# Delta rule in a scheduled two-layer kernel: key norms of four heads at once, one decay matrix per head, norms folded into columns

## Chip, cores and metric

One core of a Trainium2 chip. The metric is the device time of one execution in microseconds (us); lower is better.

## What is computed

Two layers on x of shape 512 x 2048, all in float32. Layer 0 is chunked attention beside an mLSTM; layer 1 is an RG-LRU beside a gated delta rule with 8 heads of width 128. The change touches the delta rule alone, which in the reference is (chunks of 64 there, the kernel uses chunks of 128):

```python
qkv = silu(causal_dwconv(concatenate([qd, kd, vd]), conv_d_w))
q, k = l2norm(q), l2norm(k)                     # x * rsqrt(sum(x*x) + 1e-6)
decay = cumsum(gc)                              # per chunk and head
gam = exp(where(tril, decay[t] - decay[s], NEG))
a_mat = where(strict, (k*beta)[t] . k[s] * gam, 0)
t_inv = inverse(eye + a_mat)
u, w = t_inv @ (v*beta), t_inv @ (k*beta*exp(decay))
qk = q[t] . k[s] * gam
kd = k * exp(decay[-1] - decay)
# scan over chunks: v_new = u - w@st; o = (q*exp(decay))@st + qk@v_new
#                   st = exp(decay[-1])*st + kd^T@v_new
```

## The kernel before

Every product runs on TensorE (PE) with each float32 operand split into a high and a low part, so that a product of two operands is three matmuls (lines 291 to 293, or 365 in the paired form). Layer 1 multiplies the normed input by 48 tiles of weights; each tile is 16 steps of such a triple. The program is recorded by hand in the order in which it is to run on PE, VectorE (DVE), ScalarE (ACT) and GpSimd (POOL): `Net.run` walks through units of four steps, and beside each it issues, ahead of their use, the loads of raw weights (10 units ahead, on SP's queue), the split of the weights (5 units ahead: ACT rounds to the high part, line 247, DVE subtracts, line 248) and the matmuls. After every two steps, that is six matmuls, it calls `tick`, and a tick advances each active job by one step:

```python
def tick(self):
    while len(self.active) < self.nact and self.jobs:
        self.active.append(self.jobs.popleft())
    for g in list(self.active):
        if next(g, self) is self:
            self.active.remove(g)
```

Jobs are generators that emit their instructions on all engines and then wait a number of ticks from the table LAG (`yield from self.wait("gam")`). So places in the program are counted in ticks, and each engine runs its own list in order.

The jobs of layer 1 stand in a queue (lines 1039 to 1048), of which four are active until the solve is done, then six (line 1224):

- `start1`: the norm of the rows, the gates, and `delta_gates`, which leaves columns of decay, exp(decay), exp(last decay - decay) and beta per head in `cols`.
- `delta_keys(h)`, eight of them: convolution of the keys (line 1137, three DVE operations), silu, transposes on PE (1165), the sum of squares by head (1173), a reciprocal root by Newton steps on 128x4 columns (`rsqrt_cols`, lines 623 to 629), the decay matrix with a strict triangle in `gamma` (two POOL operations 1149 and 1150, one Exp on ACT 1152), a product by a column on POOL (1188), k.k on PE (1193), the product with the decay matrix on DVE (1194), and a write of the result to DRAM (`ud`, line 1195, issued by POOL).
- `solve`: loads 32 pieces of `ud` of all heads (1207, on SP's queue), and inverts the 32x32 diagonal blocks of all heads at once by 31 steps of one product (1214) and one sum (1220) on DVE, the last on 961 elements per partition. It waits `sv`, 8 ticks, between loads and first step.
- `lru_block(n)`: the RG-LRU of one block: convolution, parts (595, 1356), six matmuls, then a chain over ACT and DVE with a scan (1378) and a gate (672, 1380).
- `inverse(h)`: blocks from the solve are put together (DVE transpose 1242, matmuls 1250 and 1257, copies); `kd` is scaled on POOL (1241).
- `delta_head(h)`: q and v convolved, a second decay matrix `att` (POOL 1278, 1279, ACT 1282, POOL 1284), q.k (1291), transpose of v (1297), then the scan over four chunks (1310 to 1329), norm and gate.

DVE thus holds, in one list, the splits that PE's next weights need (248) and the work of all jobs.

Of the kernel before, what the change touches and what calls it, by code (L numbers as in the profile page):

```python
# [52 lines left out]
for _h in range(4):  # L53
# [14 lines left out]
    "sums": 1, "sums.x0": 40, "sums.y0": 14, "sums.y1": 10, "ml.sm": 2, "vals": 4,  # L68
    "conv": 2, "gam": 8, "sv": 8,
    "sv.n": 300,  # L70
# [10 lines left out]
class Net:  # L81
# [9 lines left out]
    def __init__(self, ctx, tc, a):  # L91
# [31 lines left out]
        self.spilt = {}  # L123
        self.heads = self.turn = 0
        self.paired = {"x0", "y0", "y1"}
# [607 lines left out]
    def start0(self, raw):  # L733
# [19 lines left out]
        yield from self.lam_scale()  # L753
        self.tri1 = self.triangle(-NEG, -1)
        yield from self.wait(4)
# [259 lines left out]
    def layer1(self):  # L1015
# [23 lines left out]
        self.jobs += [self.start1()]  # L1039
        self.jobs += [self.delta_keys(h) for h in range(8)]  # L1040
        self.jobs += [self.solve()]
# [11 lines left out]
    def start1(self):  # L1053
        while ("x1", KT - 1) not in self.t and ("x1", KT - 1) not in self.x:
            yield
        self.phase.close()
        self.mp = self.phase.enter_context(self.tc.tile_pool(name="m1", bufs=1))
        self.nact = 4
        self.cols = self.mp.tile([P, 4, 4, 8], F32, name="dcols")
        self.ncols = self.mp.tile([P, 4, 8], F32, name="ncols")  # L1060

        self.kcols = self.mp.tile([P, 8, 4, 4], F32, name="kcols")
        yield from self.wait("row1")
        yield from self.row_norm(self.acc)
        g = self.gate_rows((yield from self.take("g1")))
        yield from self.delta_gates(g)
# [24 lines left out]
    def delta_gates(self, g):  # L1091
# [52 lines left out]

    def gamma(self, h, db, g, tri):

        nc = self.nc
        yield
        nc.gpsimd.tensor_tensor(self.c4(g), self.c4(db), self.mask_bc(tri), ALU.subtract)
        nc.gpsimd.tensor_tensor(self.c4(g), self.c4(g), self.col_bc(self.cols[:, 0, :, h]), ALU.subtract)  # L1150
        yield from self.wait("gam")
        nc.scalar.activation(g, g, AF.Exp)
        yield

    def delta_keys(self, h):
        nc = self.nc
        cv = yield from self.take((h, "k"))
        k = yield from self.conv(cv, C_DW + 32 + 4 * h)
        yield from self.wait("dk.silu")
        yield from self.silu2(k)  # L1160
        yield from self.wait("dk.tr")
        nc.gpsimd.dma_start(self.kfd[h], k)
        ps = self.psum("dk.tr")
        for c in range(4):
            nc.tensor.transpose(ps[:, c * P : c * P + P], k[:, c * P : c * P + P], self.ident)
        kt, g = self.ev(), self.ev()
        sq = self.tmp()
        nc.scalar.activation(kt, ps, AF.Copy)
        ss = self.small(P, 4)
        nc.scalar.activation(sq, kt, AF.Square)  # L1170
        db = self.dec_bc(h)
        yield from self.wait(2)
        nc.vector.tensor_reduce(ss, self.c4(sq), AX.X, ALU.add)
        nc.gpsimd.dma_start(self.ktd[h], kt)
        while "gates1" not in self.t:
            yield

        nc.vector.tensor_scalar(ss, ss, 4 * EPS, None, ALU.add)
        r = self.rsqrt_cols(ss)
        kc = self.kcols[:, h]  # L1180
        nc.vector.tensor_copy(kc[:, 0], r)
        nc.vector.scalar_tensor_tensor(kc[:, 1], ss, 0.5, r, ALU.mult, ALU.mult)
        nc.vector.tensor_tensor(kc[:, 2], r, self.cols[:, 3, :, h], ALU.mult)
        nc.vector.tensor_tensor(kc[:, 3], r, self.cols[:, 2, :, h], ALU.mult)
        nb = self.small(P, 4)
        nc.vector.scalar_tensor_tensor(nb, kc[:, 2], -1.0, r, ALU.mult, ALU.mult)
        yield from self.gamma(h, db, g, self.tri1)
        nc.gpsimd.tensor_tensor(self.c4(g), self.c4(g), self.col_bc(nb), ALU.mult)
        yield from self.wait("dk.kk")
        ps = self.psum("dk.kk")  # L1190
        for c in range(4):
            kc = k[:, c * P : c * P + P]
            nc.tensor.matmul(ps[:, c * P : c * P + P], kc, kc, start=True, stop=True)
        nc.vector.tensor_tensor(g, g, ps, ALU.mult)
        nc.gpsimd.dma_start(self.ud[h], g)
        self.t[(h, "u")] = True
# [29 lines left out]
    def inverse(self, h):  # L1226
# [13 lines left out]
        yield from self.wait("inv.tp")  # L1240
        nc.gpsimd.tensor_tensor(self.c4(kd), self.c4(kd), self.col_bc(self.kcols[:, h, 3]), ALU.mult)
        nc.vector.transpose(l, x)
# [23 lines left out]
    def delta_head(self, h):  # L1266
# [7 lines left out]
        db = self.dec_bc(h)  # L1274
        kc = self.kcols[:, h]
        q = yield from self.conv(cq, C_DW + 4 * h, out=q)
        nc.scalar.activation(ed, db, AF.Exp)
        nc.gpsimd.tensor_tensor(self.c4(att), self.c4(db), self.mask_bc(self.tri), ALU.subtract)
        nc.gpsimd.tensor_tensor(self.c4(att), self.c4(att), self.col_bc(self.cols[:, 0, :, h]), ALU.subtract)
        v = yield from self.conv(cv, C_DW + 64 + 4 * h, out=v)  # L1280
        yield from self.wait("gam")
        nc.scalar.activation(att, att, AF.Exp)
        yield from self.silu2(q)
        nc.gpsimd.tensor_tensor(self.c4(att), self.c4(att), self.col_bc(kc[:, 0]), ALU.mult)

# [12 lines left out]
        vt = v  # L1298
        nc.vector.tensor_tensor(self.c4(vt), self.c4(ps), self.col_bc(kc[:, 1]), ALU.mult)
        x4, kd = yield from self.take((h, "inv"))  # L1300
# [5 lines left out]
        for c in range(4):  # L1306
# [10 lines left out]
            vn = self.small(P, P, "r", 6)  # L1317
            nc.vector.tensor_scalar(vn, ps[:, :P], kc[:, 2, c : c + 1], None, ALU.mult)
            yield from self.wait("dh.kv")
# [26 lines left out]
    def lru_block(self, n):  # L1346
        nc = self.nc
        cv = yield from self.take((n, "x"))
        gw = self.mp.tile([P, 256], F32, tag="gw", name=self.uid("gw"), bufs=1)
        gp = [self.mp.tile([P, 256], F32R, tag=t, name=self.uid(t), bufs=1) for t in ("gh", "gl")]  # L1350
# [144 lines left out]
```

## Time and profile before

| what | value |
|---|---|
| median of 3 runs | 1870.02 us (1868.22 to 1870.05) |
| the profiled execution | 1869.16 us, span of its instructions 1867.3 us |
| busy share | PE 98%, DVE 73%, ACT 47%, POOL 14% |
| layer 1 | from about 1050 us to the end |

The span runs from the first to the last instruction. A busy PE is one with a matmul in flight; how fast these follow each other is seen in the timeline, where the start of one to the start of the next is its cost.

### The profile page before, as it was taken

What the parts mean: (1) busy time and instruction counts of PE and PEld (TensorE: products, weight loads), DVE (VectorE), ACT (ScalarE), POOL (GpSimd) and SP (SyncE); (2) the same over time, 40 slices, a digit from 0 to 9 for tenths busy, and PEclk for the clock granted to TensorE, in tenths of its full rate; (3) what the DMA queues carried; (4) which work ended last, traced back from release to release, by engine and by line L of the source; (5) the groups of instructions that cost most, each with busy time, mean ns of one, the idle gap of its engine ahead of it and who ended that gap; (6) DMA issues with size and microseconds to landing.
All of it is one profiled execution on the core that took longest, in us unless ns stands there. A gap on an engine that the chain in (4) does not pass through costs nothing.

```text
span 1867.3 us, 27580 instructions
## 1 busy us (share of the span) xinstructions
PE 1833.3 (98%) x10162; PEld 1567.9 (84%) x10162; DVE 1358.4 (73%) x2352; ACT 868.7 (47%) x1512; POOL 264.7 (14%) x293
## 2 busy tenths in 40 slices
PE   7999999999999999999999999999999999999999
PEld 4789889989889899988899788887788888777998
DVE  8577747797647558788777799889656666768664
ACT  4346435645435355565434544363323334566332
POOL 8101100210110101011011114201212112100000
PEclk9999999999999999999999999999999999999999
DMA  5333423333433333325644435443433333245542
GB/s 184 100 106 109 134 87 119 96 113 116 135 100 106 115 102 108 113 86 187 222 141 149 147 118 169 146 119 103 150 93 114 110 114 110 75 124 166 175 136 74
DMA packets 137287, 232.12 MB, mean 124 GB/s; under 512 B 22896, under 2 KB 32240, under 8 KB 137152
## 3 DMA queue, kind: packets, MB, share of 16 engines
q1 hardware_dynamic: 129488, 208.60, 36.8%
q0 software_dynamic: 5360, 17.57, 2.5%
q10 hardware_dynamic: 2304, 4.20, 0.6%
q8 instruction: 80, 1.31, 0.3%
q14 instruction: 55, 0.45, 0.1%
HBM read 203.79 MB, written 26.51 MB: 123 GB/s over the span
## 4 chain that ended last, share of the span: by engine, by line
PE 78%; DVE 14%; issue 3%; ACT 2%; DMA 2%; SPq 1%; DVEq 0%; ACTq 0%
PE pp L365 38%; PE pp L291 8%; PE pp L293 7%; PE pp L292 7%; DVE act L248 3%; PE pp L427 3%; PE pp L429 3%; PE pp L428 3%; DVE act L1214 1%; ACT act L247 1%; DVE act L567 1%; DVE act L1137 1%; DVE ev L1137 1%; DMA act<-in_xT 1%; SPq L1207 0%
## 5 line engine op out<-in xcount | busy, mean ns | idle before, releaser
L365 PE MATMUL pp<-act,act 128*128 128x256 f32 (+1 forms) x4884 | 794.5, 322 | 0.0
L365 PEld LDWEIGHTS pp<-act,act 128*128 128x128 f32 x4884 | 707.0, 190 | 70.2
L248 DVE TENSOR_TENSOR act<-wr,act 128x512 fp32r<-128x512 f32 x719 | 521.6, 741 | 240.6 <-ACT act L247 237.0
L247 ACT ACTIVATE act<-wr 128x512 fp32r<-128x512 f32 x719 | 418.8, 620 | 200.7 <-DVE wr L222 61.5
L291 PE MATMUL pp<-act,act 128*128 128x512 f32 x960 | 390.3, 407 | 1.3 <-ACT act L563 1.3
L293 PE MATMUL pp<-act,act 128*128 128x512 f32 x960 | 378.1, 394 | 11.8 <-DVE act L248 11.6
L292 PE MATMUL pp<-act,act 128*128 128x512 f32 x960 | 376.9, 393 | 2.7 <-DVE act L567 1.9
L293 PEld LDWEIGHTS pp<-act,act 128*128 128x128 f32 x960 | 181.4, 189 | 54.1 <-DVE act L248 15.1
L291 PEld LDWEIGHTS pp<-act,act 128*128 128x128 f32 x960 | 182.1, 190 | 40.6 <-issue 3.8
L292 PEld LDWEIGHTS pp<-act,act 128*128 128x128 f32 x960 | 181.9, 189 | 38.9 <-DVE act L567 3.2
L427 PE MATMUL pp<-act,act 128*128 128x512 f32 x256 | 100.3, 392 | 0.0
L429 PE MATMUL pp<-act,act 128*128 128x512 f32 x256 | 99.7, 390 | 0.0
L428 PE MATMUL pp<-act,act 128*128 128x512 f32 x256 | 99.7, 389 | 0.0
L222 DVE TENSOR_TENSOR wr<-wr,wr 128x512 f32<-128x512 f32 x111 | 78.0, 703 | 1.3
L980 POOL TENSOR_SCALAR pq<-pq,mx 128x512 f32<-128x512 f32 (+3 forms) x32 | 47.4, 1495 | 188.7 <-DVE mx L977 188.7
L381 ACT ACTIVATE ee<-pp 128x512 f32<-128x512 f32 x74 | 44.0, 594 | 61.5 <-PE pp L365 61.3
L528 POOL DMA_DIRECT2D yd<-ev x20 | 11.4, 568 | 401.6 <-DVE ev L1011 164.5
L784 DVE TENSOR_TENSOR ev<-ev,pp 128x512 f32<-128x512 f32 x32 | 22.0, 687 | 47.6 <-PE pp L365 43.0
L429 PEld LDWEIGHTS pp<-act,act 128*128 128x128 f32 x256 | 48.0, 188 | 10.1
L428 PEld LDWEIGHTS pp<-act,act 128*128 128x128 f32 x256 | 48.1, 188 | 9.7
L427 PEld LDWEIGHTS pp<-act,act 128*128 128x128 f32 x256 | 48.1, 188 | 9.6
L593 ACT ACTIVATE act<-ev 128x512 fp32r<-128x512 f32 x40 | 24.9, 627 | 52.3 <-DVE ev L938 31.0
(334 smaller groups left out, 2033.1 us busy)
## 6 DMA issues: line engine op xcount, KB each, us to landing
wr<-in_wi SPq DMA_DIRECT2D x216, 256.0 KB
wr<-in_ws SPq DMA_DIRECT2D x100, 256.0 KB
wr<-in_wd SPq DMA_DIRECT2D x100, 256.0 KB
wr<-in_wv SPq DMA_DIRECT2D x64, 256.0 KB
wr<-in_wso SPq DMA_DIRECT2D x48, 256.0 KB
wr<-in_wdo SPq DMA_DIRECT2D x48, 256.0 KB
wr<-in_wo SPq DMA_DIRECT2D x32, 256.0 KB
ev<-x1d SPq DMA_DIRECT2D x28, 256.0 KB
```

Of the source, the lines that this page charges most:

```text
L222: sub = lambda o, x, y: nc.vector.tensor_tensor(o, x, y, ALU.subtract)
L247: nc.scalar.activation(h, w, AF.Copy)
L248: nc.vector.tensor_tensor(l, w, h.bitcast(F32), ALU.subtract)
L291: nc.tensor.matmul(ps, h[:, j, :], xh, start=k == 0, stop=False)
L292: nc.tensor.matmul(ps, h[:, j, :], xl, start=False, stop=False)
L293: nc.tensor.matmul(ps, l[:, j, :], xh, start=False, stop=k == KT - 1)
L365: mm = lambda o, x, y, start=False: nc.tensor.matmul(o, x, y, start=start, stop=True, skip_group_check=True)
L381: nc.scalar.activation(e, ps, AF.Copy)
L427: nc.tensor.matmul(ps, xh, h, start=k == 0, stop=False)
L428: nc.tensor.matmul(ps, xh, l, start=False, stop=False)
L429: nc.tensor.matmul(ps, xl, h, start=False, stop=k == KT - 1)
L980: nc.gpsimd.tensor_scalar(rows(b), rows(b), mx[:, 3, b : b + 1], None, ALU.mult)
```

## The change

Four things. The job `delta_keys` is cut in two, `keys(h)` and `couplings(h)`; between them stands `key_norms`, once for heads 0 to 3 and once for 4 to 7, which does the Newton steps on 128x16 columns of four heads. The decay matrix is made once per head: one POOL subtraction (1195), four Exps of 128x128 on ACT with the decay column as bias (1198), written to DRAM (`gd`) by POOL; `delta_head` loads it from there on SP's queue in place of making its own. The norms are no longer multiplied into matrices on POOL: they enter as columns, in four 128x128 DVE evictions of k.k (1207), and in column products that were there already; `kd` is scaled by four ACT operations. And `lru_block` waits until the block before it has issued its matmuls; the queue of jobs has a new order.

```diff
-    "conv": 2, "gam": 8, "sv": 8,
+    "conv": 2, "gam": 5, "dk.db": 3, "dh.q": 6, "sv": 8,
...
-        self.jobs += [self.delta_keys(h) for h in range(8)]
+        self.jobs += [self.keys(h) for h in range(4)] + [self.key_norms(0)]
+        self.jobs += [f(h + 4 * i) for h in range(4) for i, f in ((1, self.keys), (0, self.couplings))]
+        self.jobs += [self.key_norms(4)] + [self.couplings(h) for h in range(4, 8)]
...
+        nc.vector.tensor_scalar(self.ndec, self.cols[:, 0], -1.0, None, ALU.mult)
...
-    def gamma(self, h, db, g, tri):
-
-        nc = self.nc
-        yield
-        nc.gpsimd.tensor_tensor(self.c4(g), self.c4(db), self.mask_bc(tri), ALU.subtract)
-        nc.gpsimd.tensor_tensor(self.c4(g), self.c4(g), self.col_bc(self.cols[:, 0, :, h]), ALU.subtract)
-        yield from self.wait("gam")
-        nc.scalar.activation(g, g, AF.Exp)
-        yield
...
-        nc.vector.tensor_reduce(ss, self.c4(sq), AX.X, ALU.add)
+        nc.vector.tensor_reduce(self.kcols[:, 0, h], self.c4(sq), AX.X, ALU.add)
         nc.gpsimd.dma_start(self.ktd[h], kt)
+        self.t[h, "ss"] = True
+
+    def key_norms(self, h0):
+
+        nc = self.nc
+        yield from self.take(*((h, "ss") for h in range(h0, h0 + 4)))
         while "gates1" not in self.t:
             yield
-
-        nc.vector.tensor_scalar(ss, ss, 4 * EPS, None, ALU.add)
-        r = self.rsqrt_cols(ss)
...
-        yield from self.gamma(h, db, g, self.tri1)
-        nc.gpsimd.tensor_tensor(self.c4(g), self.c4(g), self.col_bc(nb), ALU.mult)
+        half, b, nb = [self.kcols[:, i, h0 : h0 + 4] for i in range(3)]
+        flat = half.rearrange("p h c -> p (h c)")
+
+        nc.vector.tensor_scalar(flat, flat, 4 * EPS, None, ALU.add)
+        r = self.rsqrt_cols(flat).rearrange("p (h c) -> p h c", c=4)
...
+    def couplings(self, h):
+
+        nc = self.nc
+        yield from self.take((h, "norms"))
+        db, k, g = self.dec_bc(h), self.ev(), self.ev()
+        nc.sync.dma_start(k, self.kfd[h])
+        yield from self.wait("dk.db")
+        nc.gpsimd.tensor_tensor(self.c4(db), self.c4(db), self.mask_bc(self.tri), ALU.subtract)
+        yield from self.wait("gam")
+        for c in range(4):
+            nc.scalar.activation(self.c4(g)[:, c], self.c4(db)[:, c], AF.Exp, bias=self.ndec[:, c, h : h + 1])
+        nc.gpsimd.dma_start(self.gd[h], g)
         yield from self.wait("dk.kk")
         ps = self.psum("dk.kk")
+        u = db
         for c in range(4):
             kc = k[:, c * P : c * P + P]
             nc.tensor.matmul(ps[:, c * P : c * P + P], kc, kc, start=True, stop=True)
-        nc.vector.tensor_tensor(g, g, ps, ALU.mult)
-        nc.gpsimd.dma_start(self.ud[h], g)
+        for c in range(4):
+            nc.vector.scalar_tensor_tensor(self.c4(u)[:, c], self.c4(ps)[:, c], self.kcols[:, 2, h, c : c + 1], self.c4(g)[:, c], ALU.mult, ALU.mult)
+        nc.gpsimd.dma_start(self.ud[h], u)
...
-        nc.gpsimd.tensor_tensor(self.c4(kd), self.c4(kd), self.col_bc(self.kcols[:, h, 3]), ALU.mult)
+        for c in range(4):
+            nc.scalar.activation(self.c4(kd)[:, c], self.c4(kd)[:, c], AF.Copy, scale=self.cols[:, 2, c, h : h + 1])
...
+        nc.sync.dma_start(att, self.gd[h])
         q = yield from self.conv(cq, C_DW + 4 * h, out=q)
         nc.scalar.activation(ed, db, AF.Exp)
-        nc.gpsimd.tensor_tensor(self.c4(att), self.c4(db), self.mask_bc(self.tri), ALU.subtract)
-        nc.gpsimd.tensor_tensor(self.c4(att), self.c4(att), self.col_bc(self.cols[:, 0, :, h]), ALU.subtract)
         v = yield from self.conv(cv, C_DW + 64 + 4 * h, out=v)
-        yield from self.wait("gam")
-        nc.scalar.activation(att, att, AF.Exp)
+        yield from self.wait("dh.q")
         yield from self.silu2(q)
-        nc.gpsimd.tensor_tensor(self.c4(att), self.c4(att), self.col_bc(kc[:, 0]), ALU.mult)
...
         cv = yield from self.take((n, "x"))
+        while self.lrus < n:
+            yield
...
         self.product(i, [t[:, P:] for t in gp], xp)
+        self.lrus += 1
```

Since lists and waits in ticks set the order, two places show what moved. The first is POOL's list where the last of the eight `ud` is written, ahead of the solve. Before, a write stands after the work of its own head:

```order
L1188 TENSOR_TENSOR ev_11504<-ev_11504,sm_11555 128x512
L1174 DMA ktd<-ev_11653 128x512
L1149 TENSOR_TENSOR ev_11654<-tmp_11659,tri_1106 128x512
L1150 TENSOR_TENSOR ev_11654<-ev_11654,dcols 128x512
L1195 DMA ud<-ev_11504 128x512
L1188 TENSOR_TENSOR ev_11654<-ev_11654,sm_11712 128x512
L1195 DMA ud<-ev_11654 128x512
L1208 MEMSET act_11907 128x1024
```

With the change the four heads of the second group come together, and their writes stand in a row:

```order
L1199 DMA gd<-ev_11564 128x512
L1208 DMA ud<-tmp_11537 128x512
L1208 DMA ud<-tmp_11551 128x512
L1208 DMA ud<-tmp_11556 128x512
L1208 DMA ud<-tmp_11561 128x512
L1221 MEMSET act_11748 128x1024
L1222 MEMSET act_11748 128x32
```

The writes of heads 4 to 7 now leave POOL one after the other, and the memset for the solve follows at once. The second place is DVE's list at steps 20 to 22 of the solve (lines 1214 and 1220 before, 1227 and 1233 in the change; 248 are the splits for PE, 365 to 378 and 1378 to 1391 the RG-LRU, 1141 a convolution). Before:

```order
L1214 TENSOR_TENSOR act_11908<-act_11906,act_11907 128x400
L1220 TENSOR_REDUCE act_11907<-act_11908 128x20
L248 TENSOR_TENSOR act_12331<-wr_12241,act_12331 128x512
L1214 TENSOR_TENSOR act_11908<-act_11906,act_11907 128x441
L1220 TENSOR_REDUCE act_11907<-act_11908 128x21
L1365 TENSOR_SCALAR act_12356<-act_12356,spl 128x512
L1366 SCALAR_TENSOR_TENSOR ev_12185<-act_12356,ev_12185 128x512
L248 TENSOR_TENSOR act_12363<-wr_12267,act_12363 128x512
L481 TENSOR_TENSOR cv_12382<-pp_12295,rb 128x512
L1214 TENSOR_TENSOR act_11908<-act_11906,act_11907 128x484
L1220 TENSOR_REDUCE act_11907<-act_11908 128x22
L1373 SCALAR_TENSOR_TENSOR act_12356<-act_12356,tmp_12372 128x512
```

With the change:

```order
L1227 TENSOR_TENSOR act_11749<-act_11747,act_11748 128x400
L1233 TENSOR_REDUCE act_11748<-act_11749 128x20
L1378 TENSOR_SCALAR act_12144<-act_12144,spl 128x512
L1379 SCALAR_TENSOR_TENSOR ev_11963<-act_12144,ev_11963 128x512
L248 TENSOR_TENSOR act_12157<-wr_12050,act_12157 128x512
L1227 TENSOR_TENSOR act_11749<-act_11747,act_11748 128x441
L1233 TENSOR_REDUCE act_11748<-act_11749 128x21
L1386 SCALAR_TENSOR_TENSOR act_12144<-act_12144,tmp_12166 128x512
L1141 SCALAR_TENSOR_TENSOR ev_12153<-cv_11813,cst,ev_12153 128x512 x3
L248 TENSOR_TENSOR act_12185<-wr_12074,act_12185 128x512
L1227 TENSOR_TENSOR act_11749<-act_11747,act_11748 128x484
L1233 TENSOR_REDUCE act_11748<-act_11749 128x22
```

Before, steps 20 to 22 stand beside the chain of one RG-LRU block; with the change a convolution of the next block stands there as well. From the first step of the solve to the first transpose of `inverse` (1242, now 1256) DVE's list holds, beside the 62 operations of the solve, before 33 splits, 5 convolutions of three operations, 3 scans and 30 other operations, 3 of them short (line 1365, or 256 columns); with the change 33 splits, 7 convolutions, 4 scans and 38 others, 7 of them short. Up to the point at which the solve has ended and one gate has followed (line 672, the last operation ahead of 1314.02 in the trace), before holds 25 of the splits, 3 of the convolutions, the 3 scans and 26 of the others.

## Rows read from the trace of the kernel before

**Rows 1.** The page: busy time and share of the span by engine.

```profile
PE 1833.3 (98%) x10162; PEld 1567.9 (84%) x10162; DVE 1358.4 (73%) x2352; ACT 868.7 (47%) x1512; POOL 264.7 (14%) x293
```

**Rows 2.** Waits of PE, 1060 to 1760 us: who, for whom; us, times, longest.

```profile
PE pp L293 <- DVE act L248: 3.3, 2, 2.2
...
PE dh_kv L1322 <- DVE r L1318: 0.7, 1, 0.7
```

**Rows 3.** Windows of layer 1: width; PE, PEld, DVE, ACT, POOL busy; clock; DMA.

```profile
1180.00:1200.00 20.00, 18.74 (x94) 15.49 (x92) 18.97 (x52) 3.99 (x8) 7.34 (x10) 1.00 0.43 138
1280.00:1300.00 20.00, 16.66 (x66) 13.00 (x65) 19.72 (x24) 5.53 (x10) 5.96 (x8) 0.92 0.29 92
1300.00:1320.00 20.00, 17.65 (x76) 14.41 (x76) 18.76 (x20) 5.08 (x10) 8.93 (x6) 0.90 0.60 187
```

**Rows 4.** Timeline of PE: start us, us, instruction, [idle before <-releaser].

```profile
1185.64 0.63 PE L1165 MATMUL dk_tr<-ident,ev 128*128 128x128 f32 x4 [1.26 <-DVE ev L672]
...
1211.61 1.05 PE L1193 MATMUL dk_kk<-ev 128*128 128x128 f32 x8
...
1224.16 0.39 PE L291 MATMUL pp<-act,act 128*128 128x512 f32 x1
...
1288.85 0.39 PE L291 MATMUL pp<-act,act 128*128 128x512 f32 x1
...
1295.82 0.50 PE L293 MATMUL pp<-act,act 128*128 128x512 f32 x1 [2.19 <-DVE act L248]
...
1298.00 0.63 PE L291 MATMUL pp<-act,act 128*128 128x512 f32 x1
1298.43 0.63 PE L292 MATMUL pp<-act,act 128*128 128x512 f32 x1
...
1314.16 1.11 PE L1297 MATMUL dh_vt<-ident,act 128*128 128x128 f32 x4 [2.35 <-DVE act L672]
```

**Rows 5.** Timeline of DVE before and at the solve; columns as in rows 4.

```profile
1217.25 1.22 DVE L1378 TENSOR_TENSOR_SCAN ev<-act,ev 128x512 f32<-128x512 f32 x1
...
1220.31 2.32 DVE L1137 SCALAR_TENSOR_TENSOR ev<-cv,cst,ev 128x512 f32<-128x512 f32 x3
...
1224.48 0.48 DVE L1365 TENSOR_SCALAR act<-act,spl 128x512 f32<-128x512 f32 x1
1224.88 0.68 DVE L1366 SCALAR_TENSOR_TENSOR ev<-act,ev 128x512 f32<-128x512 f32 x1
1225.48 0.69 DVE L248 TENSOR_TENSOR act<-wr,act 128x512 fp32r<-128x512 f32 x1
...
1231.65 0.16 DVE L1214 TENSOR_TENSOR act<-act,act 128x1 f32<-128x1 f32 x1 [3.34 <-DMA act<-ud]
```

**Rows 6.** Groups of DVE, 1231 to 1314 us: count, busy us, mean ns, idle before.

```profile
L1214 DVE TENSOR_TENSOR act<-act,act 128x1 f32<-128x1 f32 (+30 forms) x31 | 24.3, 783 | 3.5 <-DMA act<-ud 3.3
...
L1220 DVE TENSOR_REDUCE act<-act 128x1 f32<-128x1 f32 (+30 forms) x31 | 15.6, 503 | 1.1
```

**Rows 7.** Timeline of DVE beside POOL instructions; columns as in rows 4.

```profile
1286.98 2.98 DVE L1137 SCALAR_TENSOR_TENSOR act<-cv,cst,act 128x512 f32<-128x512 f32 x3
...
1314.02 4.67 DVE L248 TENSOR_TENSOR act<-wr,act 128x512 fp32r<-128x512 f32 x3
...
1503.19 4.42 DVE L1137 SCALAR_TENSOR_TENSOR act<-cv,cst,act 128x512 f32<-128x512 f32 x3
```

**Rows 8.** The 32 loads of the solve on SP’s queue (timeline).

```profile
1213.76 16.14 SPq L1207 DMA_DIRECT2D act<-ud  x32
```

**Rows 9.** Line 1195, the writes of ud: ns min/median/max; time to landing.

```profile
L1195 POOL DMA_DIRECT2D ud<-ev x8: 539/562/586, 1132.5 to 1216.2; - x8
...
DMA to landing us min/median/max: 3.4/4.1/6.3
```

**Rows 10.** ACT, groups by shape: a 128x128 Exp with a column as bias.

```profile
L855 ACT ACTIVATE pk<-tmp,ccol 128x128 f32<-128x128 f32 x16 | 6.2, 389 | 0.0
```

**Rows 11.** Groups of DVE, 1095 to 1216 us; columns as in rows 6.

```profile
L628 DVE TENSOR_SCALAR sm<-sm 128x4 f32<-128x4 f32 x24 | 7.2, 299 | 0.8
```

More of the change, by code (lines that the diff above doesn't have):

```diff
@@ L123, in __init__ @@
         self.spilt = {}
-        self.heads = self.turn = 0
+        self.heads = self.turn = self.lrus = 0
         self.paired = {"x0", "y0", "y1"}
@@ L753, in start0 @@
         yield from self.lam_scale()
-        self.tri1 = self.triangle(-NEG, -1)
         yield from self.wait(4)
@@ L1020, in layer1 @@
         self.ud = self.dr.tile([8, P, S], F32, name="ud")
+        self.gd = self.dr.tile([8, P, S], F32, name="gd")
         self.xd = self.dr.tile([P, 32, 32], F32, name="xd")
@@ L1060, in start1 @@
         self.ncols = self.mp.tile([P, 4, 8], F32, name="ncols")
-        self.kcols = self.mp.tile([P, 8, 4, 4], F32, name="kcols")
+        self.ndec = self.mp.tile([P, 4, 8], F32, name="ndec")
+        self.kcols = self.mp.tile([P, 3, 8, 4], F32, name="kcols")
         yield from self.wait("row1")
@@ L1143, in dec_bc, with keys @@
         return t
-    def gamma(self, h, db, g, tri):
-        nc = self.nc
-        yield
-        nc.gpsimd.tensor_tensor(self.c4(g), self.c4(db), self.mask_bc(tri), ALU.subtract)
-        nc.gpsimd.tensor_tensor(self.c4(g), self.c4(g), self.col_bc(self.cols[:, 0, :, h]), ALU.subtract)
-        yield from self.wait("gam")
-        nc.scalar.activation(g, g, AF.Exp)
-        yield
-    def delta_keys(self, h):
+    def keys(self, h):
         nc = self.nc
@@ L1165, in delta_keys @@
             nc.tensor.transpose(ps[:, c * P : c * P + P], k[:, c * P : c * P + P], self.ident)
-        kt, g = self.ev(), self.ev()
+        kt = self.ev()
         sq = self.tmp()
         nc.scalar.activation(kt, ps, AF.Copy)
-        ss = self.small(P, 4)
         nc.scalar.activation(sq, kt, AF.Square)
-        db = self.dec_bc(h)
         yield from self.wait(2)
-        nc.vector.tensor_reduce(ss, self.c4(sq), AX.X, ALU.add)
+        nc.vector.tensor_reduce(self.kcols[:, 0, h], self.c4(sq), AX.X, ALU.add)
@@ L1174, in delta_keys @@
         nc.gpsimd.dma_start(self.ktd[h], kt)
+        self.t[h, "ss"] = True
+    def key_norms(self, h0):
+        nc = self.nc
+        yield from self.take(*((h, "ss") for h in range(h0, h0 + 4)))
         while "gates1" not in self.t:
             yield
-        nc.vector.tensor_scalar(ss, ss, 4 * EPS, None, ALU.add)
-        r = self.rsqrt_cols(ss)
-        kc = self.kcols[:, h]
-        nc.vector.tensor_copy(kc[:, 0], r)
-        nc.vector.scalar_tensor_tensor(kc[:, 1], ss, 0.5, r, ALU.mult, ALU.mult)
@@ L1183, in delta_keys @@
[L1183 to L1186, printed above, removed]
-        yield from self.gamma(h, db, g, self.tri1)
-        nc.gpsimd.tensor_tensor(self.c4(g), self.c4(g), self.col_bc(nb), ALU.mult)
+        half, b, nb = [self.kcols[:, i, h0 : h0 + 4] for i in range(3)]
+        flat = half.rearrange("p h c -> p (h c)")
@@ new lines, in key_norms @@
+        nc.vector.tensor_scalar(flat, flat, 4 * EPS, None, ALU.add)
+        r = self.rsqrt_cols(flat).rearrange("p (h c) -> p h c", c=4)
+        nc.vector.tensor_tensor(b, r, r, ALU.mult)
+        nc.vector.scalar_tensor_tensor(half, half, 0.5, r, ALU.mult, ALU.mult)
+        nc.vector.tensor_tensor(b, b, self.cols[:, 3, :, h0 : h0 + 4].rearrange("p c h -> p h c"), ALU.mult)
+        nc.vector.tensor_scalar(nb, b, -1.0, None, ALU.mult)
+        for h in range(h0, h0 + 4):
+            self.t[h, "norms"] = True
@@ L1274, in delta_head @@
         db = self.dec_bc(h)
-        kc = self.kcols[:, h]
+        nc.sync.dma_start(att, self.gd[h])
         q = yield from self.conv(cq, C_DW + 4 * h, out=q)
         nc.scalar.activation(ed, db, AF.Exp)
-        nc.gpsimd.tensor_tensor(self.c4(att), self.c4(db), self.mask_bc(self.tri), ALU.subtract)
-        nc.gpsimd.tensor_tensor(self.c4(att), self.c4(att), self.col_bc(self.cols[:, 0, :, h]), ALU.subtract)
         v = yield from self.conv(cv, C_DW + 64 + 4 * h, out=v)
-        yield from self.wait("gam")
-        nc.scalar.activation(att, att, AF.Exp)
+        yield from self.wait("dh.q")
         yield from self.silu2(q)
-        nc.gpsimd.tensor_tensor(self.c4(att), self.c4(att), self.col_bc(kc[:, 0]), ALU.mult)
         nc.scalar.activation(qs, q, AF.Square, scale=0.128)
@@ L1298, in delta_head @@
         vt = v
-        nc.vector.tensor_tensor(self.c4(vt), self.c4(ps), self.col_bc(kc[:, 1]), ALU.mult)
+        nc.vector.tensor_tensor(self.c4(vt), self.c4(ps), self.col_bc(self.kcols[:, 0, h]), ALU.mult)
         x4, kd = yield from self.take((h, "inv"))
@@ L1317, in delta_head @@
             vn = self.small(P, P, "r", 6)
-            nc.vector.tensor_scalar(vn, ps[:, :P], kc[:, 2, c : c + 1], None, ALU.mult)
+            nc.vector.tensor_scalar(vn, ps[:, :P], self.kcols[:, 1, h, c : c + 1], None, ALU.mult)
             yield from self.wait("dh.kv")
```

## Prediction

> **What bounds the kernel now.** I read the page's busy shares first: PE is busy for 1833.3 us of a span of 1867.3, 98%, DVE 73%, ACT 47%, POOL 14% [rows 1]. Work taken off DVE, ACT or POOL is worth something only where PE waits for it, so I next read PE's waits in layer 1: two waits for DVE's split of the weights (line 248), 3.3 us together, and smaller ones in the heads, such as 0.7 at line 1322 [rows 2]. Then the windows: DVE is busy 18.97 of 20 us beside the key jobs and 19.72 beside the solve, where PE's granted clock falls to 0.92 and then 0.90; beside the key jobs it is 1.00 [rows 3]. Two levels are mixed there: at 1298.00 a matmul follows the one before after 0.43 us, where the rate is otherwise 0.23, that is 1.2 and not 2.4 GHz, and this comes just behind an idle time of 2.19 us [rows 4].
>
> PE's rate without a stall: 285 matmuls, all of 512 columns, lie between 1224.16 and 1288.85 [rows 4], so one costs 64.69 / 285 = 0.227 us and a tick of six 1.36.
>
> DVE is a list run in order. Up to 1217.25 its lead over PE is good; then the first operation of the solve stands idle for 3.34 us on the loads of `ud` and starts at 1231.65 [rows 5], while the tick it belongs to began on PE at 1224.16 [rows 4]: 7.5 us late. Every split behind it is late too. The solve itself is long (31 products of 24.3 us and 31 sums of 15.6, together 39.9 [rows 6]), so nothing is made up, until PE stalls: at 1295.82 for the split and at 1314.16, with 2.35, for a gate [rows 4]. So the time is set by PE's rate plus what DVE is late at the solve.
>
> **What is lost now.** From the first solve operation to 1314.02 DVE needs 82.4 us [rows 5, 7]. In the same stretch PE has 57 ticks (77.6), two RG-LRU products of six matmuls (2.8) and 0.8 of small products: 81.2. DVE is then late by 7.5 + 82.4 - 81.2 = 8.7. PE's losses agree: 3.3 to 3.7 of waits for splits [rows 2], 2.4 at 1314.16, the rest in matmuls at the lower clock, each 0.43 - 0.23 = 0.2 dearer.
>
> **The change part by part.** Prices of DVE from start to start: 0.60 for a 512-wide split or other operation (1224.88 to 1225.48), 0.40 for a short one, 1.22 for a scan, 2.32 for a convolution [rows 5].
>
> *The norms of four heads at once.* Removed: eight chains of about 20 DVE operations of 128x4, 299 ns each by the sample [rows 11]; added: two chains of the same length on 128x16. Net some 120 operations, 36 us less of DVE, all ahead of the solve. There PE lost to DVE only 1.26 us at 1185.64, waiting for a silu ahead of the key transposes [rows 4]. With DVE relieved I take this as gone, with 0.1 around it: **-1.4**. The rest of the 36 us is lead that DVE has anyway by 1217. The column chain becomes one wait for four heads, but all jobs of the group stand behind it in ticks, not PE.
>
> *The decay matrix once per head.* POOL loses its two big operations per matrix, and the two products by columns; ACT gains 32 Exps of 128x128 at 389 ns [rows 10] and as many copies for `kd`, for which I use the same price: 25 us at most over 250, less the 16 wide Exps that go, where ACT is busy 4.0 to 5.5 of 20 [rows 3]. Hidden, and at worst worth nothing to PE either way: a coupling's Exps stand several ticks ahead of its use. The 24 added transfers of 256 KB (eight writes of `gd`, eight loads of it, eight loads of the transposed keys) go where 0.29 to 0.60 of the DMA time is used [rows 3]; hidden. On SP's queue 16 of them stand among the loads of weights, ten units ahead of use. POOL's eight added issues cost 0.56 each [rows 9] and nothing waits for them but what is told under the rivals.
>
> *DVE beside POOL.* Three convolution operations take 2.32 us alone [rows 5] and 2.98 to 4.42 beside a POOL operation, three splits 4.67 in place of 1.8 [rows 7]. With the POOL operations gone these 2 us each come back to DVE. In the heads DVE has lead at nearly all such places; PE's wait of 0.7 [rows 2] follows one: **-0.7**. In the solve's stretch it is in the sum below.
>
> *k.k evicted in four pieces.* 32 operations of 128x128 in place of 8 of 128x512. The nearest row, 299 ns for a column operation [rows 11], and 0.60 for a 512-wide one are the ends: between +5 and +14 us of DVE over 100, paid from the 36 above.
>
> *The order of jobs and the RG-LRU in series.* This is the term that decides. The list between the first step of the solve and the first transpose of `inverse` has by the prices above: before, 39.9 + 33 x 0.60 + 5 x 2.32 + 3 x 1.22 + 27 x 0.60 + 3 x 0.40 = 92.4; with the change, 39.9 + 33 x 0.60 + 7 x 2.32 + 4 x 1.22 + 31 x 0.60 + 7 x 0.40 = 102.2. So 9.8 us of convolutions and RG-LRU move in between. The same prices give for the shorter stretch up to 1314.02 before 80.5 against 82.4 measured; part of the 1.9 more was contention with POOL that goes, so I add 1.3: 103.5. PE has in the new stretch 70 ticks (95.3) and four RG-LRU products of 1.4: 100.9.
>
> What remains is how late the first step is. Before, the last k.k was at 1211.61 [rows 4], and its write, the loads on SP (32 in 16.14 us, 0.50 each [rows 8]) and their landing put the first step at 1231.65. With the change the four last writes follow in a row, so some 24 loads of 0.50, 12 us, still go out behind the first of them, and write and load land 3.4 to 6.3 us after issue [rows 9]; the wait `sv` is 8 ticks as before. I get 6.8 to 8.8 us behind the tick and take 7.5, the value of before. DVE then is late by 7.5 + 103.5 - 100.9 = 10.1, against 8.7: **+1.4**. I expect it as some 5 us at the gates' product of an RG-LRU block (its operand, line 595 or 1368, is in the list nine ticks ahead at most) and the rest ahead of the first matmuls of `inverse`, with matmuls of 0.43 behind either.
>
> **Sum:** -1.4 - 0.7 + 1.4 = -0.7. The profiled execution took 1869.16, 0.9 below the median of 1870.02; -0.7 gives 1868.5 for such an execution and **1869.3** as median. What this kernel's measurement can tell from no change is 0.2%, 3.7 us. Unsure by +-2: the first step; by +-2.5: prices of the 145 list entries; so this case alone holds 1865.5 to 1873.
>
> **Rivals.**
>
> *The solve starts in time.* If the relieved DVE and the grouped writes bring the loads home early enough that the first step stands no more than 2 us behind its tick, the lateness is 2 + 103.5 - 100.9 = 4.6, 4.1 less than now: with the other terms -1.4 - 0.7 - 4.1 = -6.2. If the lower clock that follows each stall goes as well (1.3 us more behind 1314.16, six or seven matmuls by 0.2), and the 1.3 of contention, it is **1861.2**. For it: heads 4 to 7 share one norm chain, and three of four writes may land early. Against it: loads and `sv` are as before, and 9.8 us of list are new. Chance 0.25.
>
> *The last four writes hold up the loads.* Place: POOL's queue at the end of the couplings. Each issue takes 0.56 [rows 9], so the last write leaves up to 1.7 later than alone, and if it lands after 6.3 instead of 3.4 us [rows 9], 2.9 more is lost. Price: 1.7 + 2.9 = 4.6, which PE pays one for one since DVE has no idle time until `inverse`, and one more phase of the lower clock, 1.3: 1869.3 + 5.9 = **1875.2**. It decides from a first step over 11 us behind its tick. Against it: all eight landings of before lie between 3.4 and 6.3 with DVE busy 18.97 of 20 us [rows 3, 9], so a full DVE did not lengthen them beyond that. The Trainium skill ("SBUF — State Buffer", section "Who interferes with whom") says that a DMA issued through GpSimd can starve while DVE holds the port the two share, and that DMAs otherwise never contend with an engine. By that rule the writes in a row, issued while DVE is full, would land at the long end, which is this rival; the landings of before bear it out only in their spread. Chance 0.20.
>
> *The likeliest case* keeps 0.55: stalls move, their sum hardly does.
>
> **How the numbers follow.** Faster by over 0.2% (below 1866.3): nearly all of the first rival, 0.23, and 0.08 of the likeliest. Slower (above 1873.8): 0.16 of the second and 0.05 of the likeliest. Same: 0.48. The range 1861.0 to 1875.0 cuts the first rival and the second about in half, 0.12 and 0.09.
>
> **What would show it.** Right: no wait at the key transposes; the first step of the solve idle for several us on `ud`, 6 to 9 behind its tick; a wait of PE of some 5 us at an RG-LRU gates' product and one at the first matmuls of `inverse`; a granted clock below 1 in that stretch again; DVE's convolutions in the heads at 2.3 us. Wrong: PE busy and the clock at 1.00 all through 1270 to 1330 (the first rival), a first step over 11 us late (the second), or PE waiting for ACT's Exps, for a load of `gd`, or for weights, to all of which I gave nothing.

## The result and the profile after

The changed kernel takes 1881.36 us (median of 4, 1879.19 to 1882.18), the kernel before timed beside it 1869.78: a ratio of 1.0062, 95% interval 1.0046 to 1.0078. It is slower by 11.6 us, where 1869.3 with a range of 1861.0 to 1875.0 was forecast, and lies above that range.

The profiled execution took 1882.18 us, with a span of 1880.4. The page's first part, which answers to [rows 1]:

```profile
PE 1844.7 (98%) x10162; PEld 1577.8 (84%) x10162; DVE 1317.3 (70%) x2255; ACT 880.2 (47%) x1560; POOL 205.2 (11%) x251
```

DVE has 41 us less and POOL 60 us less than before, ACT 12 more: the change did to the engines' load what its parts say. PE, the bound, is busy for 11.4 us longer with the same 10162 instructions. The waits of PE between 1060 and 1760 us (columns as in [rows 2]) tell where:

```profile
PE dh_ks L1320 <- DVE r L1335: 4.9, 3, 3.0
PE dh_kv L1332 <- DVE r L1328: 4.7, 2, 4.5
PE inv_z L1264 <- DVE act L1256: 4.0, 1, 4.0
PE lru_r L602 <- DVE act L595: 2.7, 1, 2.7
PE pp L293 <- DVE act L248: 0.7, 1, 0.7
```

The third to fifth are the solve's stretch, where [rows 2, 4] had two waits for splits and one for a gate. The first two are new: the scan over chunks of a head (`dh_ks`, `dh_kv`) waits for DVE 300 us after the solve. [rows 2] shows one such wait of 0.7 for the kernel before; with three lines more of the same view it had 3.3 us of them in five waits, none over 1.2. Windows of the changed kernel (columns as in [rows 3]):

```profile
1180.00:1200.00 20.00, 20.00 (x96) 16.70 (x95) 15.52 (x33) 11.39 (x28) 8.33 (x11) 1.00 0.76 279
...
1280.00:1300.00 20.00, 16.61 (x65) 12.86 (x64) 19.76 (x26) 11.57 (x18) 1.58 (x4) 0.91 0.25 79
1300.00:1320.00 20.00, 20.00 (x89) 16.54 (x89) 18.73 (x24) 11.92 (x18) 0.69 (x3) 1.00 0.62 196
1320.00:1340.00 20.00, 16.00 (x115) 12.77 (x114) 16.25 (x30) 9.26 (x23) 0.00 (x0) 0.83 0.58 180
1600.00:1620.00 20.00, 16.78 (x86) 12.72 (x85) 11.72 (x24) 4.92 (x12) 0.58 (x1) 0.74 0.28 81
1640.00:1660.00 20.00, 15.50 (x66) 12.72 (x65) 12.40 (x23) 11.65 (x17) 0.58 (x1) 0.83 0.26 78
```

and of the kernel before in the last two:

```profile
1600.00:1620.00 20.00, 19.93 (x129) 15.81 (x127) 13.70 (x27) 7.38 (x15) 1.68 (x3) 1.00 0.35 100
1640.00:1660.00 20.00, 19.43 (x97) 16.06 (x95) 11.30 (x20) 12.01 (x19) 0.65 (x2) 1.00 0.29 87
```

From 1600 to 1620 PE runs 86 matmuls where it ran 129, while DVE is busy for only 11.72 of 20 us. So DVE is not short of time there; it stands in its own list waiting for something. PE pays twice, for the wait and for matmuls at the lower clock (granted 0.74 and 0.83) behind it. The two long waits in PE's timeline (columns as in [rows 4]):

```profile
1608.89 0.80 PE L1320 MATMUL dh_ks<-r,act 128*128 128x128 f32 x2 [3.03 <-DVE r L1335]
1646.39 0.79 PE L1332 MATMUL dh_kv<-r,act 128*128 128x128 f32 x2 [4.50 <-DVE r L1328]
```

To add this up I go through PE's timeline and, for each 512-wide matmul of layer 1 whose successor starts over 0.1 us later than the usual 0.235, sum the excess. That is PE's loss. It gives 20.6 us for the kernel before and 32.2 after. The difference, 11.6, is as large as that of the medians; the spans of the two profiled executions differ by 13.1, of which 0.7 had come about before layer 1 began, where the change touches nothing.

| PE's loss, us | 1060 to 1260 (keys) | 1260 to 1345 (solve) | 1345 to 1675 (heads) | from 1675 |
|---|---|---|---|---|
| before | 2.6 | 9.3 | 5.9 | 2.8 |
| after | 1.6 | 11.6 | 18.1 | 1.0 |

Keys, solve and the end nearly cancel, as forecast. The heads lose 12.2 us more, and the forecast had -0.7 there. (The table is read from one profiled execution of each kernel.) What DVE's list does at the first of the two places (timeline of DVE, columns as in [rows 4]):

```profile
1603.39 0.31 DVE L1328 TENSOR_SCALAR r<-dh_xr,kcols 128x128 f32<-128x128 f32 x1
1603.62 0.68 DVE L672 SCALAR_TENSOR_TENSOR act<-tmp,act 128x512 f32<-128x512 f32 x1
1606.56 0.69 DVE L248 TENSOR_TENSOR act<-wr,act 128x512 fp32r<-128x512 f32 x1 [2.26 <-ACT act L247]
1607.17 0.68 DVE L672 SCALAR_TENSOR_TENSOR ev<-tmp,ev 128x512 f32<-128x512 f32 x1
1607.89 0.69 DVE L1353 TENSOR_TENSOR act<-act,ev 128x512 f32<-128x512 f32 x1
1608.50 0.34 DVE L1335 SCALAR_TENSOR_TENSOR r<-r,act,dh_kv 128x128 f32<-128x128 f32 x1
```

and ACT's timeline beside it:

```profile
1604.33 0.63 ACT L1296 ACTIVATE act<-act 128x512 f32<-128x512 f32 x1 [2.92 <-DVE act L672]
1604.87 0.62 ACT L670 ACTIVATE tmp<-act 128x512 f32<-128x512 f32 x1
1605.39 0.61 ACT L593 ACTIVATE act<-ev 128x512 fp32r<-128x512 f32 x1
1605.91 1.66 ACT L247 ACTIVATE act<-wr 128x512 fp32r<-128x512 f32 x3
```

Two lists in order cross. ACT waits 2.92 us for DVE's gate of the next head's q (672) to square it (1296); behind the square stand two more operations and the rounding of weights (247); DVE waits 2.26 for that rounding to do its split; and behind the split stands the state update of the running head (1335), whose input, the product at 1603.76, was long there. PE then starts the product of line 1320 at 1608.89, after 3.03 us of idle time. In the kernel before, the same update (1325 there) ran at 1604.71 and the gate of q came after it, at 1605.95:

```profile
1604.71 0.34 DVE L1325 SCALAR_TENSOR_TENSOR r<-r,act,dh_kv 128x128 f32<-128x128 f32 x1
...
1605.95 1.37 DVE L672 SCALAR_TENSOR_TENSOR act<-tmp,act 128x512 f32<-128x512 f32 x1
```

The second place is of the same kind: `dh_xr` runs on PE at 1638.74, and the operation for it (1328) starts at 1645.99, behind the chain of RG-LRU block 4, part of which waits for a square root on ACT:

```profile
1641.30 0.69 DVE L1390 TENSOR_TENSOR ev<-ev,act 128x512 f32<-128x512 f32 x1 [1.25 <-ACT act L1388]
1642.03 1.22 DVE L1391 TENSOR_TENSOR_SCAN ev<-act,ev 128x512 f32<-128x512 f32 x1
1643.17 2.30 DVE L1141 SCALAR_TENSOR_TENSOR ev<-cv,cst,ev 128x512 f32<-128x512 f32 x3
1645.39 0.68 DVE L248 TENSOR_TENSOR act<-wr,act 128x512 fp32r<-128x512 f32 x1
1645.99 0.34 DVE L1328 TENSOR_SCALAR r<-dh_xr,kcols 128x128 f32<-128x128 f32 x1
```

Why do they meet now? Counted in ticks of the list, the scans of all heads come two ticks earlier than before (the solve starts that much earlier), and the products q.k of heads 2 to 7 four ticks earlier (`dh.q` is 6 where the wait ahead of the gate of q was 8). RG-LRU blocks 4 to 7 stand at the same ticks as before, since the tiles of weights that feed them set their start.

### The profile page after: what moved, and what is told of

It reads as the page before. It is cut to its first block, busy times and chain, and to the rows that moved or that the text cites. A ratio compares the mean times of both kernels' runs of the same rounds, so it can differ in the third digit from the quotient of the medians.

```text
span 1880.4 us, 27524 instructions
## 1 busy us (share of the span) xinstructions
PE 1844.7 (98%) x10162; PEld 1577.8 (84%) x10162; DVE 1317.3 (70%) x2255; ACT 880.2 (47%) x1560; POOL 205.2 (11%) x251
## 4 chain that ended last, share of the span: by engine, by line
PE 82%; DVE 10%; issue 3%; ACT 2%; DMA 1%; SPq 1%; DVEq 0%; ACTq 0%; POOLq 0%
PE pp L365 38%; PE pp L291 9%; PE pp L293 9%; PE pp L292 8%; PE pp L427 3%; PE pp L429 3%; PE pp L428 3%; DVE act L248 3%; DVE act L1227 1%; DVE act L567 1%; DMA act<-in_xT 1%; ACT act L247 1%; PE inv_z L1264 1%; DMA wr<-in_wi 0%; SPq L1220 0%
## 5 line engine op out<-in xcount | busy, mean ns | idle before, releaser
L248 DVE TENSOR_TENSOR act<-wr,act 128x512 fp32r<-128x512 f32 x719 | 515.7, 732 | 281.2 <-ACT act L247 278.5
L528 POOL DMA_DIRECT2D yd<-ev x20 | 11.4, 569 | 458.9 <-DVE ev L1010 164.5
```

What stands on the lines that cost most here:

```text
L248: nc.vector.tensor_tensor(l, w, h.bitcast(F32), ALU.subtract)
```

## Experiments

Two theories. **PHASE**: the 12 us come from where the heads' steps fall in the lists against splits, gates and RG-LRU chains, two to four ticks off; the new work in the heads costs nothing. **CONTENT**: the new work (four ACT copies for `kd`, the decay matrix loaded from DRAM) delays the lists. Each run was timed beside the kernel before in five rounds.

### heads_as_before

```diff
-    "conv": 2, "gam": 5, "dk.db": 3, "dh.q": 6, "sv": 8,
+    "conv": 2, "gam": 5, "dk.db": 3, "dh.q": 8, "sv": 8,
...
-        yield from self.wait("dh.first")
+        yield from self.wait("dh.first" if h else 5)
```

> The changed kernel with two waits of the heads altered: dh.q 8 in place of 6, and the wait ahead of the first head's scan 5 in place of 4. By the list, every product of the heads then stands at the same tick as in the kernel before, and the rest of the change stays. Theory PHASE (the 12 us lost in the heads come from where the heads' steps fall against the RG-LRU chain of blocks 4 to 7 and the splits, two to four ticks earlier than before): the stalls at lines 1320 and 1332 go, PE loses 4 to 7 us between 1340 and 1670 in place of 18, time 1868 to 1872. Theory CONTENT (the new work inside the heads, four ACT copies for kd and the load of the decay matrix, delays DVE's list): the stalls stay, 1879 to 1883.

Measured: 1868.37 us, ratio 0.9998 (0.9990 to 1.0007). PE's loss in the heads is 3.4. Counted in PE's list, all products of the scans now stand at the tick of the kernel before, and q.k does from head 1 on; head 0's q.k is 20 ticks later than there (18 in the changed kernel) and the inverses of heads 0 and 1 are 2 earlier. All 12 us are gone with two numbers of waits, and the new work of the change is still there. CONTENT is out.

### before_heads_moved

The other way round: the kernel before with 6 in place of `"gam"` (8) in `delta_head`, and 2 in place of 4 for the first head's scan.

> The kernel before with the waits of the heads set the other way: 6 ticks in place of 8 ahead of the second decay matrix and the gate of q, and 2 in place of 4 ahead of the first head's scan. By the list, every product of the heads then stands at the tick it has in the changed kernel; nothing else of the change is in it. PHASE: stalls of several us at lines 1310 and 1322 near 1600 and 1640, 1876 to 1884. CONTENT: as before, 1868 to 1871, or at most 1 us of shorter margins.

Measured: 1882.52 us, ratio 1.0077 (1.0063 to 1.0091), that is 13.9 over the kernel before beside it (1868.62). Its PE timeline:

```profile
1610.20 0.49 PE L1310 MATMUL dh_ks<-r,act 128*128 128x128 f32 x2 [3.03 <-DVE r L1325]
1643.64 0.77 PE L1322 MATMUL dh_kv<-r,act 128*128 128x128 f32 x2 [4.53 <-issue]
```

These are the two stalls of the changed kernel, of 3.03 and 4.50 us, in a kernel that has none of its new operations. The heads lose 18.5 us. So two waits alone, put into the old kernel, cost as much as the change did.

### scan_later and q_later

Each half alone: the first head's scan two ticks later (6 in place of 4), or `dh.q` 8 (which moves q.k by three ticks and the scans by one).

> The changed kernel with only the first head's scan two ticks later (6 in place of 4 ticks), so that all scans stand at the ticks of the kernel before, and the gates of q still two ticks ahead of it. PHASE, second half: the stall of 4.5 us at line 1332 near 1641 (DVE's operation stands behind the sum and scan of RG-LRU block 4, which wait for ACT) goes, with its slow matmuls, some 6 us; the one near 1605 stays or shrinks: 1870 to 1877. CONTENT: 1879 to 1883.

Measured: 1874.87 us, ratio 1.0037 (1.0024 to 1.0050); the heads lose 9.2 us. Against the kernel before timed beside it, the changed kernel is 11.6 us slower, this one 6.2, and heads_as_before 0.2 faster. So about half of the cost goes with the place of the scans. The 4.5 us at line 1332 shrinks to 1.6, the other kind stays:

```profile
PE dh_ks L1320 <- DVE r L1335: 3.6, 3, 2.5
```

> The changed kernel with dh.q 8 in place of 6 alone: the gate of q and the product q.k come three ticks later, the scan one tick later. PHASE, first half: the stall of 3.0 us at line 1320 near 1605 (DVE's state update stands behind the gate of q and a split that waits for ACT) goes, with its slow matmuls, some 6 us; the stall of 4.5 near 1641 goes only if one tick is enough: 1872 to 1877. CONTENT: 1879 to 1883.

Measured: 1870.28 us, ratio 1.0008 (1.0000 to 1.0017); the heads lose 6.0. That is 1.7 us over the kernel before, faster than expected: for the second stall one tick of the scans was nearly enough. This edit alone takes away some 10 of the 11.6 us and scan_later alone some 5, so the two do not simply add.

### kd_on_pool

heads_as_before with `kd` scaled as before, by one POOL product instead of four ACT copies:

> heads_as_before with kd scaled by one POOL product as in the kernel before, in place of four ACT copies. If POOL beside DVE is what the change took away in the heads (my term of 0.7): DVE operations of twice the length near the eight products again, 1869 to 1871. If ACT's four copies (1.27 us of ACT per head) hold up splits: up to 2 us faster, 1866 to 1868. If neither: 1868 to 1869.

Measured: 1869.51 us, ratio 0.9997 (0.9987 to 1.0006), the heads losing 3.4. By its ratio this is the same as heads_as_before (0.9998). The time itself lies in the first band, but the kernel before, timed beside it, was 1.0 us slower too (1869.64, against 1868.62 beside heads_as_before). So for the time as a whole it is neither, and there is no evidence here for my term for POOL beside DVE in the heads. In the solve's stretch the trace has a little: one convolution operation takes 1.45 us beside a product on POOL where 0.75 is usual, and the stretch loses 13.2 in place of 12.1.

### solve_later and before_solve_later

In the solve's stretch the change costs 2.3 us more. DVE sits idle for 6.04 us ahead of the solve's first step, until `ud` has landed, where before had 3.34 [rows 5]:

```profile
1217.63 0.69 DVE L248 TENSOR_TENSOR act<-wr,act 128x512 fp32r<-128x512 f32 x1
1224.36 0.16 DVE L1227 TENSOR_TENSOR act<-act,act 128x1 f32<-128x1 f32 x1 [6.04 <-DMA act<-ud]
```

The edit, for heads_as_before and for the kernel before: `"sv": 8` becomes 12, and the first head's scan follows its inverse sooner (2 ticks; 0 in the kernel before), so that the scans of all heads keep their ticks.

> heads_as_before with the wait ahead of the solve's first step 12 ticks in place of 8 (and the first head's scan 2 ticks behind its inverse in place of 5, so that the heads keep their ticks). Theory LATENESS (PE's loss between 1260 and 1345, 12 us, is the 6.5 us by which the first step is behind its tick plus what the list is longer than PE's work): four ticks, 5.4 us, of the lateness go, so the loss falls to 5 to 8 us and the time to 1862 to 1865. Rival LENGTH (DVE's work in the stretch is what counts, whenever it starts, since the steps now sit four ticks later against the inverse, which is later too): the loss stays 10 us or more, 1867 to 1871.

Measured: 1864.31 us, ratio 0.9971 (0.9960 to 0.9983); the stretch loses 7.0 in place of 12.1. The first step now runs at 1229.22 with no wait right ahead of it. But the idle time has not gone; it stands three operations earlier, ahead of a split, and is longer:

```profile
1227.41 0.69 DVE L248 TENSOR_TENSOR act<-wr,act 128x512 fp32r<-128x512 f32 x1 [8.55 <-ACT act L247]
```

ACT's rounding for this split (247) had itself stood idle for 9.62 us until the raw weights landed (`wr`). In the changed kernel it is the same:

```profile
1198.71 23.39 SPq L1220 DMA_DIRECT2D act<-ud  x32
1222.21 3.20 SPq L215 DMA_DIRECT2D wr<-in_wi  x7
1225.90 1.94 ACT L247 ACTIVATE act<-wr 128x512 fp32r<-128x512 f32 x3 [9.32 <-DMA wr<-in_wi]
```

The 32 loads of `ud` stand on SP's queue for 23.39 us, where they took 16.14 before [rows 8], and the loads of weights stand behind them. In the kernel before, ACT waited only 1.23 us there.

> The kernel before with the same: 12 in place of 8 ticks ahead of the solve's first step, and the first head's scan 0 in place of 4 ticks behind its inverse, so that the heads keep their ticks. LATENESS: the loss between 1260 and 1345 falls from 9.3 to 3 to 6 us, 1863 to 1866. LENGTH: 1867 to 1870.

Measured: 1865.78 us, ratio 0.9980 (0.9971 to 0.9989); 5.9 in place of 9.3. Here the list's next work does fill the wait: the 3.34 is gone, the first step runs at 1233.60, and it is 3.5 us behind its own tick where it was 7.5.

Both times fall as LATENESS said, by 5.1 and 3.4 us of the stretch's loss. But its quantity is wrong for the changed kernel: in solve_later the first step is 5.4 us behind its own tick (1229.22 against 1223.84) where it was 6.3 in heads_as_before, so only 1 us of lateness went for 5.1 of loss. What else gave the rest was not followed; the edit also moves the inverses of heads 0 and 1 four ticks later, and PE's wait at line 1264 falls from 3.9 to 0.3.

### solve_much_later

`"sv": 16`, and the first head's scan right behind its inverse; the heads then come two ticks later than before.

> solve_later with 16 ticks in place of 12, and the first head's scan right behind its inverse; the heads then come 2 ticks later than in the kernel before. LATENESS: the solve's stretch loses 0 to 4 us; PHASE: the heads lose something else, by their place against the RG-LRU chain, between 2 and 12 us: 1858 to 1872. LENGTH: 1867 or more.

Measured: 1871.40 us, ratio 1.0013 (1.0004 to 1.0022). The stretch loses 7.7, no less than with 12 ticks, although the first step is now only 2.1 us behind its tick; DVE's idle time ahead of a split is still there (8.44). So the lateness of the first step does not set the loss by itself. The heads lose 8.5 and the end 7.6. I take this for the phase again, now off on the other side; which operations met was not followed.

### conv_later and both_later

The new order puts the convolutions of heads 0 and 1 right ahead of the transposes of `inverse` (1256). One line in `delta_head` moves those of head 1 behind them:

```diff
+        yield from self.wait(10 if h == 1 else 0)
         q = yield from self.conv(cq, C_DW + 4 * h, out=q)
```

> heads_as_before with the two convolutions of the second head (q and v, six DVE operations, 2 x 2.24 us) ten ticks later, so that they stand behind the transposes of inverse instead of ahead of them; all scans keep their ticks. Theory LENGTH OF LIST (the convolutions and RG-LRU work that the new order puts into the solve's stretch are what the stretch lost more than before): the wait of 3.9 us at line 1264 and the slow matmuls behind it go, the loss between 1260 and 1345 falls from 12.1 to 6 to 8 us, 1862.5 to 1865.5. Rival (the inverse waits for its own data, DRAM writes and loads behind the solve): the loss stays above 10, 1867 to 1870.

Measured, on heads_as_before: 1861.51 us, ratio 0.9958 (0.9945 to 0.9970). The stretch loses 6.4 in place of 12.1. PE's waits, heads_as_before first:

```profile
PE inv_z L1264 <- DVE act L1256: 3.9, 1, 3.9
PE lru_r L602 <- DVE act L595: 2.7, 1, 2.7
```

and conv_later:

```profile
PE lru_r L602 <- DVE act L595: 2.7, 1, 2.7
PE pp L293 <- DVE act L248: 1.3, 1, 1.3
```

The wait of 3.9 us at line 1264 is gone, and with it the slow matmuls: the granted clock from 1320 to 1340 is 1.00 where it was 0.83 in the changed kernel:

```profile
1320.00:1340.00 20.00, 20.00 (x167) 16.03 (x166) 17.91 (x33) 9.39 (x21) 0.00 (x0) 1.00 0.56 192
```

This is the lowest median of the study: 8.4 us under the kernel before (1869.88 beside it) and 20 under the changed one, with three numbers of waits. (both_later, below, is not clearly slower: the intervals overlap.)

> solve_later and conv_later together. If lateness at the first step and length of the list add up: the loss between 1260 and 1345 falls from 7.0 to 2 to 4 us, 1860 to 1863. If they take away the same stall: 1863 to 1866.

Measured: 1862.88 us, ratio 0.9965 (0.9951 to 0.9978). The gains do not add; the stretch loses 6.7. With the solve four ticks later the moved convolutions run between the transposes of `inverse` and its next DVE operation (1266), and a new wait of 3.04 stands at line 1271:

```profile
1333.07 1.55 PE L1271 MATMUL inv_t<-act,tmp 32*32 32x32 f32 x32 [3.04 <-issue]
```

What each kernel loses, by stretch:

| PE's loss, us | keys | solve | heads | end | median us |
|---|---|---|---|---|---|
| heads_as_before | 1.2 | 12.1 | 3.4 | 3.7 | 1868.37 |
| q_later | 1.2 | 12.4 | 6.0 | 2.3 | 1870.28 |
| scan_later | 1.2 | 12.0 | 9.2 | 3.6 | 1874.87 |
| before_heads_moved | 2.7 | 8.0 | 18.5 | 1.0 | 1882.52 |
| kd_on_pool | 1.6 | 13.2 | 3.4 | 2.8 | 1869.51 |
| solve_later | 1.9 | 7.0 | 3.4 | 2.7 | 1864.31 |
| before_solve_later | 2.7 | 5.9 | 5.5 | 2.8 | 1865.78 |
| solve_much_later | 1.2 | 7.7 | 8.5 | 7.6 | 1871.40 |
| conv_later | 1.2 | 6.4 | 3.4 | 3.6 | 1861.51 |
| both_later | 1.2 | 6.7 | 3.5 | 2.8 | 1862.88 |

Not separated: what the norms of four heads bring by themselves, apart from POOL's relief, and the wait of `lru_block` for the block before it. Not tried: letting the loads of weights pass those of `ud` on SP's queue.

## Why the prediction was wrong

**The step that failed** is the one for the heads. The prediction said "In the heads DVE has lead at nearly all such places", gave them -0.7, and priced the order of jobs only between the first step of the solve and `inverse`. That `dh.q` is 6 where 8 stood, and that the scans come two ticks earlier, was in the diff and in the lists, and got no term at all. It was worth +12.2. Lead was the wrong quantity to judge this by: 11.30 or 13.70 us of DVE work in 20, as in the two windows of the kernel before above, says that DVE has time, but the scan of a head is a chain PE, DVE, PE, whose DVE operations stand in one list with operations that wait for ACT. The margin of each depends on its place, and two ticks, 2.7 us, were enough to lose it (1868.62 against 1882.52 in before_heads_moved). None of the rivals named this mechanism, so the range could not hold it: the slower rival had another place and ended at 1875.2.

**The keys** (-1.4): right in size. No wait at the key transposes; the loss there falls from 2.6 to 1.2 in most runs (1.6 in the changed kernel's profile). PE is busy 20.00 us from 1180 to 1200 where it was 18.74 [rows 3]. Which part of the change did it was not separated.

**The solve's stretch** (+1.4): right in place and nearly in size. It measured +2.3, and +2.8 in heads_as_before. DVE took 104.0 us from the first step to the transposes (1224.36 to 1328.39) against 103.5 forecast; 1.47 of them is idle time of DVE for ACT's rounding, behind the late weights. The forecast gave nothing to the queue of weights: PE never waited for it directly, but ACT did, for 9.32 us, and DVE behind ACT. The first step was 6.5 us behind its tick (PE's tick began at 1217.86) against 7.5. The stalls came where they were expected, at the gates' product of an RG-LRU block (2.66, with some 5 forecast) and ahead of `inverse` (4.00), with the lower clock behind both. conv_later shows that convolutions ahead of the transposes are what PE waits for at the second of these: the order of jobs, which this term priced.

**POOL beside DVE** (-0.7): not shown either way. The convolutions in the heads do take 2.3 us, and with the heads at their old ticks the loss there is 3.4 against 5.9 before, but putting one POOL product per head back left it at 3.4. The change also has a new case of the same kind, at the keys, where the four subtractions of a group now stand in a row on POOL:

```profile
1187.09 5.48 DVE L627 TENSOR_TENSOR sm<-sm,kcols 128x16 f32<-128x16 f32 x1
1187.47 5.06 POOL L1195 TENSOR_TENSOR tmp<-tmp,tri 128x512 f32<-128x512 f32 x4
1193.22 0.18 DVE L627 TENSOR_TENSOR sm<-sm,kcols 128x16 f32<-128x16 f32 x1
```

The same operation of line 627 that takes 0.18 us at 1193.22 took 5.48 beside the four, and ended when they did. PE did not wait for it (it is busy for the whole 20 us from 1180 to 1200), so it cost nothing here.

**k.k in four pieces**: 32 operations of 344 ns in the trace, which overlap and keep DVE busy for 8.8 us; the eight of 680 before took 5.4. These 3.4 us more are below the +5 to +14 I gave, and hidden. The writes landed in 2.3 to 5.0 us, also with four in a row, and the first step was 6.5 us late, so the rival on POOL's queue did not come about. The Trainium skill's rule on starved descriptors ("SBUF — State Buffer", "Who interferes with whom") is not borne out here, but it was not put to a hard test either: DVE was busy only 11.31 of 20 us at that place.

```profile
1200.00:1220.00 20.00, 20.00 (x106) 17.13 (x105) 11.31 (x28) 2.90 (x6) 3.39 (x8) 1.00 0.33 95
```

**As a whole** the forecast fits the change with the heads left at their ticks: 1869.3 forecast, 1868.37 measured. Part of this fit is luck. Against the kernel before, heads_as_before loses 1.4 less in the keys, 2.8 more in the solve's stretch, 2.5 less in the heads and 0.9 more at the end, where the forecast had -1.4, +1.4, -0.7 and nothing.

## What to carry to other kernels

When the order of work is set by waits in ticks, list every chain between engines whose ticks move against work that does not move, and read the margin of each of its steps in the list; a low busy share says nothing of it. A change that removes work and moves its neighbours is two changes: put the places back first, as heads_as_before did, and only then judge the work. And when a job that waits for DRAM is made to start later, look at the whole list again: in before_solve_later the idle time was filled, in solve_later it came back ahead of a split, since the weights stood behind the same loads on one queue.

## What was not expected of the hardware

A stall of PE can cost more than its length. The 3.03 us at 1608.89 in the changed kernel was followed by a granted clock that averages 0.74 from 1600 to 1620, with fifteen 512-wide matmuls at 0.43 us or more in place of 0.23, the lower of the clock's two levels. The same stall of 3.03 us in before_heads_moved was followed by none: its window reads

```profile
1600.00:1620.00 20.00, 16.25 (x105) 12.63 (x105) 13.93 (x27) 6.18 (x13) 1.36 (x2) 1.00 0.29 86
```

In that kernel's heads the clock fell only behind the stall of 4.53. So the length of the wait alone does not tell whether the lower clock follows, and the price of one and the same stall differs by some 3 us (fifteen times 0.2). What else decides was not tried.
